# Merged additions for the compressed keys and values, and a different split of the PSUM banks, in a fused two-mixer transformer block

## The chip, the core and the metric

The kernel runs on one core of a Trainium2 chip. TensorE (PE in the profile) does the matrix multiplications and writes its results to PSUM, which has eight banks of 128 x 512 floats. VectorE (DVE) and ScalarE (ACT) read PSUM and do elementwise work, GpSimd (POOL) does elementwise work on SBUF alone, SyncE (SP) issues most DMAs. The metric is device time in microseconds (us), the median of several runs.

## The reference, cut to what matters

A block of x (512 tokens, width 1024) goes through a first mixer (an mLSTM branch and a stick-breaking attention branch), an MLP, and then a second mixer, "NSA": 16 heads of 64 in 4 key groups, and three attention branches (compressed, selected, window) that are gated and summed. The change lies in the second mixer. What it computes there:

```python
def compress_kv(kv, pos, w1, w2):        # 31 blocks of 32 tokens, one every 16 tokens
    blocks = kv[:, idx] + pos            # each block, plus a learned position table
    flat = blocks.reshape(B, n_cmp, G, CMP_BLOCK * dh)
    return jax.nn.silu(flat @ w1) @ w2   # done for the keys (k_c) and for the values (v_c)

kc, vc = compress_kv(k_c, ...), compress_kv(v_c, ...)
o_cmp, p_cmp = nsa_compressed(q, kc, vc, table)
o_slc = nsa_selected(q, k_s, v_s, sel, table)
o_win = nsa_window(q, k_w, v_w, table)
y = sum(gates * stack([o_cmp, o_slc, o_win]) * silu(z))   # z: three projections of width 1024
```

With 512 tokens the selected branch takes all 8 blocks and the window covers all tokens, so both are causal softmax attention over everything.

## The kernel before, in words

A float32 product is made of float32r parts: every operand is split into a high part and a remainder (`hi_lo`, or `Weights._load` for weights), and each product is three matmuls, high x high, low x high and high x low. In the trace a projection is therefore groups of three 128 x 512 matmuls on L339, L340 and L341 (`gen_t`, 24 matmuls into one PSUM bank), followed by `evac`, which reads the bank.

The second mixer (`nsa`) is written as an interleaving. `attention` walks through 8 head pairs, 2 branches, 2 heads and 4 blocks of queries. Each step issues the scores of one block (L1217 and L1218, into the ring of banks `sc`), then the transposes of an earlier block's probabilities ("flips", L1237, into the ring `tp`; ScalarE and VectorE copy them out to `ptall`), then the value product of a finished half (L1253, bank `av`). Between these a `Filler` puts pieces of other work, three matmuls at a time: the projections for the next queries, keys and the gates z (`project`, `queries`, `keys`), and the compressed branch (`compress`, `cmp_hidden`, `cmp_scores`, `cmp_flip`). These take their banks from `pj` or `mx`, which are one and the same ring, `bank`. The Filler's budget is counted in fixed costs, so the order of instructions on TensorE and GpSimd is settled when the program is built (`manual_schedule`); VectorE and ScalarE are ordered by the compiler's scheduler. All engines run in order.

A ring hands its banks out in turn, whoever asks. A matmul that opens a new tile in a bank waits until the last reader of the bank's previous tile is through. For a projection of z that reader is `evac` in `project`: ScalarE writes tanh(bank/2) to z (L995), then VectorE forms (z + 1) * bank (L296, in `stt`). For queries it is two ScalarE/VectorE pairs (L875 and L296).

`compress(i)` (i = 0 for keys, 1 for values) projects two 128-row halves, copies each to an SBUF tile (`kv`, L901), and while the next projection `project(0, i + 1)` runs, it builds four blocks F_ of shifted copies plus positions, eight additions of 64 x 4 x 31 each (`block`, L299 in `tt`), all eight at once at every second step. Each block is then split into Fh (ScalarE, L924) and Fl (GpSimd), and `cmp_hidden` multiplies the four (L942 to L944) into a bank of `pj`, interleaved with another projection by `both`.

Of the kernel before, what the change touches and what calls it, by code (L numbers as in the profile page):

```python
# [8 lines left out]
F32 = mybir.dt.float32  # L9
F32R = mybir.dt.float32r  # L10
# [5 lines left out]
T = 512  # L16
# [8 lines left out]
ZB = 5  # L25
# [220 lines left out]
def emit(gen):  # L246
    for _ in gen:
        pass
# [3 lines left out]
def tile_blocks(ctx, tc, x, xt, wts, prm, cst, table, post_g, w2k, w2v, out):  # L252
# [19 lines left out]
    ident = glob.tile([128, 128], F32, name="ident")  # L272
    ones = glob.tile([128, 128], F32, name="ones")
    v.memset(ones, 1.0)
    warm = glob.tile([128, 128], F32, name="warm", tag="dg", bufs=2)
    s.activation(warm, ones, AF.Identity, scale=ones[:, 0:1])
    wb = ring(7)()
    for _ in range(WARM):
        pe.matmul(wb[:, 0:128], ones, ones, start=True, stop=True)
    mhalf = glob.tile([128, 32], F32, name="mhalf")  # L280
# [34 lines left out]

    def row_broadcast(psum, r, name, scale=None):
        ps = psum()
        for tb in range(4):
            dg = glob.tile([128, 128], F32, name="dg", tag="dg", bufs=2)
            ts(dg, ident, r[:, tb:tb + 1])  # L320
            pe.matmul(ps[:, 128 * tb:128 * tb + 128], ones, dg, start=True, stop=True)
        o = glob.tile([128, T], F32, name=name, tag="rb", bufs=1)
        s.copy(o, ps)
        return o
# [70 lines left out]
    def first_mixer():  # L395
        with tc.tile_pool(name="pa", bufs=1) as pa:
            pj, sc, mx, tp, av = ring(0, 1, 2, 3), ring(4), ring(5), ring(6), ring(7)
            acts = []
# [18 lines left out]
            with tc.tile_pool(name="pm", bufs=1) as pm:  # L417
# [25 lines left out]
                with tc.issue_after(first.ins):  # L443
                    R = row_broadcast(mx, rs, "rbc")
                fa = pa.tile([8, T], F32, name="fa", tag="w2", bufs=2)
# [45 lines left out]
                for j in range(4):  # L491
# [16 lines left out]
                    for e in range(2):  # L508
# [33 lines left out]
                        for half in range(2):  # L542
# [7 lines left out]
                            v.tensor_copy(num[:, 2 * half:2 * half + 2, :], o2)  # L550
                        jk = glob.tile([128, 128], F32, name="jk", tag="dg", bufs=2)
                        for tb in range(4):
# [228 lines left out]
    def nsa(x2, ssq2):  # L781
# [4 lines left out]
        with ExitStack() as pts:  # L786
            pt = pts.enter_context(tc.tile_pool(name="pt", bufs=1))
            bank, sc, tp, av = ring(0, 1, 7), ring(2, 3), ring(4, 5), ring(6)

# [56 lines left out]

            def tmp(name="w"):
                return pt.tile([128, T], F32, name=name, tag="w", bufs=2)

            def keys_evac(gq):  # L850
                def evac(ps):
                    ks = tmp("ks")
                    s.copy(ks, ps)  # L853
                    for br in range(2):
                        kh = pn.tile([128, T], F32R, name="kh", tag="kh", bufs=4)
                        kl = pn.tile([128, T], F32R, name="kl", tag="kl", bufs=4)
                        src = ks[64 * br:64 * br + 64, :]
                        same = slice(64 * br, 64 * br + 64)
                        for d_ in range(2):
                            s.copy(kh[64 * d_:64 * d_ + 64, :], src)  # L860
                        for d_ in range(2):
                            tt(kl[64 * d_:64 * d_ + 64, :], src, kh[same, :].bitcast(F32), OP.subtract)
                        kst[gq, br] = (kh, kl)
                return evac
# [18 lines left out]
            def values(br):  # L883
                def evac(tb, ps):
                    src = ps[:, 0:256].rearrange("p (g d) -> p g d", g=4)
                    hi = vst[:, tb, 4 * br:4 * br + 4, 0:64]
                    gs = gn[:, tb, 24 * br:24 * br + 24]
                    s.activation(gs, ps[:, 256:280], AF.Tanh, scale=0.5)
                    ts(gs, gs, 0.25, 0.25, OP.mult, OP.add)
                    s.copy(hi, src)  # L890
                    tt(vst[:, tb, 4 * br:4 * br + 4, 64:128], src, hi.bitcast(F32), OP.subtract)
                emit(gen_n((ring(3, 4, 5, 6), ring(2, 0, 1, 7))[br], acts, evac, w=280))
                if br == 0:
                    ts(gn[:, 0, 0:16], gn[:, 0, 0:16], valid)

            def compress(i, hooks=((), ())):
                src = []

                def evac(ps):
                    t_ = tmp("kv")  # L900
                    s.copy(t_, ps)  # L901
                    src.append(t_)
                for m in range(2):
                    yield from weave(gen_t(pj, acts, evac), hooks[m])
                w2 = pt.tile([128, 2, 128 if i == 0 else 64], F32, name="w2", tag="pct", bufs=1)
# [3 lines left out]

                def block(j1, j2):  # L910
                    F_ = pt.tile([128, 4, 4, 32], F32, name="F_", tag="z", bufs=ZB)
                    tc.keep_in_program_order(g.memset(F_[:, :, :, 31:32], 0.0))
                    for gq in range(4):
                        r0 = 64 * (gq % 2)
                        kvv = src[gq // 2][r0:r0 + 64, :].rearrange("p (c j b) -> p b j c", j=8, b=2)
                        for jj in range(2):
                            p0 = base + 16 * jj + 8 * j1 + 4 * j2
                            tt(F_[64 * jj:64 * jj + 64, :, gq, 0:31],
                               kvv[:, jj, 4 * j2:4 * j2 + 4, j1:j1 + 31],
                               pr[r0:r0 + 64, p0:p0 + 4, None].to_broadcast([64, 4, 31]), OP.add)  # L920
                    Fh = pn.tile([128, 4, 128], F32R, name="Fh", tag="qy", bufs=QB)
# [3 lines left out]
                    tt(Fl, src_, Fh.bitcast(F32), OP.subtract, eng=g)  # L925
                    Fs.append((Fh, Fl))
                for k, ns in enumerate(project(0, i + 1)):
                    if k % 2 == 0:
                        block(k // 4, k // 2 % 2)
                    yield ns  # L930
# [22 lines left out]
            def cmp_middle(th):  # L953
                pst = mx()
                for k in range(2):
# [7 lines left out]
            def cmp_output(i, hT, w2):  # L963
                o = mx()
                for k in range(2):
# [8 lines left out]
                else:  # L974
                    vc = glob.tile([128, 128], F32, name="vc", tag="dg", bufs=2)[:, 0:64]
                    v.tensor_copy(vc, o[:, 0:64])
# [155 lines left out]
            def gate_flip(p):  # L1132
                pst = tp()
                for tb in range(4):
                    pe.transpose(pst[:, 128 * tb:128 * tb + 128], gz[:, 8 * tb:8 * tb + 128].bitcast(F32), ident)
                o = pt.tile([128, T], F32R, name="gT", tag="w", bufs=2)
                s.copy(o, pst)
# [124 lines left out]
            def attention(fill):  # L1262
# [70 lines left out]
                while pend_flip or pend_mix:  # L1333
# [6 lines left out]
            first = [(pj(), W.next(1), keys_evac(0)), (pj(), W.next(1), queries_evac(0)),  # L1340
                     (mx(), W.next(1), queries_evac(1))]
            enter(0)
# [110 lines left out]
```

## Time and profile before

| what | value |
|---|---|
| median of 3 runs | 1370.8 us (1369.51 to 1370.91) |
| the profiled execution | 1372.04 us, span 1370.3 us |
| PE busy, share of the span | 1324.2 us, 97% |
| DVE / ACT / POOL busy | 53% / 48% / 20% |

The profile lists the busy time of PE by stretch. Up to 430 us (first mixer) it is 415.4 us; from 430 to 875 us (mostly the MLP) 444.9 of 445; from 875 to 948 us (start of the second mixer) 69.7 of 73; from 948 to 1040 us (attention with the compressed branch) 78.8 of 92; from 1040 to 1330 us (attention with the remaining projections) 281.4 of 290; and in the last 40.3 us 33.9. PEclk is the TensorE clock that was granted: 1.00 is 2.4 GHz and 0.50 is 1.2 GHz.

A timeline row gives start (us from the span's start), duration in us, engine, line, operation, out<-in, sizes; in square brackets the idle time before it and what ended it. The names `b` are PSUM banks without their number.

### The profile page before, as it was taken

Reading aid. Unit: us, or ns where it says so; the run is one execution under the profiler, and the core shown is the slowest. Engines: PE = TensorE matmul, PEld = TensorE weight load, DVE = VectorE, ACT = ScalarE, POOL = GpSimd, SP = SyncE. Lnnn points to the kernel's source line nnn. Section 1 sums busy time; section 2 is a strip of 40 time slices with the busy share of each in tenths; the row PEclk is TensorE's granted clock in tenths of the full one; section 3 lists DMA queues with packets and bytes.
Section 4 is the critical chain, followed back from the end, with each engine's and each line's share of the span. In section 5 each row is a group of like instructions: output and inputs, shape, how many; then the busy total and the mean of one; then the engine's idle time right before and its main releaser. Section 6 shows DMA issues by size and latency. Waiting matters only on the chain.

```text
span 1370.3 us, 17904 instructions
## 1 busy us (share of the span) xinstructions
PE 1324.2 (97%) x6670; PEld 1090.5 (80%) x6670; DVE 728.0 (53%) x1386; ACT 656.0 (48%) x1281; POOL 273.7 (20%) x243
## 2 busy tenths in 40 slices
PE   9999999999999999999999999999888999999998
PEld 7977887777786888888888888888667788888776
DVE  4689435656567535342233322545785766665623
ACT  6588624544434326351135512355556556665532
POOL 0023101110101000000000000145536344335342
PEclk9999999999999999999999999999999999999999
DMA  7411221213131424863333324323313122211132
GB/s 236 139 46 49 76 93 55 85 62 93 51 103 47 155 61 133 125 183 94 96 102 93 95 94 129 118 64 119 94 55 111 52 63 62 70 62 63 47 108 77
DMA packets 40695, 125.31 MB, mean 91 GB/s; under 512 B 4528, under 2 KB 9184, under 8 KB 40352
## 3 DMA queue, kind: packets, MB, share of 16 engines
q1 hardware_dynamic: 39696, 119.98, 27.7%
q0 software_dynamic: 912, 4.19, 2.3%
q8 instruction: 52, 0.85, 0.3%
q14 instruction: 35, 0.29, 0.1%
HBM read 115.77 MB, written 8.39 MB: 91 GB/s over the span
## 4 chain that ended last, share of the span: by engine, by line
PE 66%; issue 15%; DVE 10%; ACT 5%; POOL 2%; DMA 1%; SPq 0%; POOLq 0%; DVEq 0%; ACTq 0%
PE b L374 9%; PE b L372 9%; PE b L373 9%; PE b L339 9%; PE b L340 9%; PE b L341 9%; PE b L1253 2%; PE b L1237 2%; DVE b L1220 1%; DVE ptall L299 1%; ACT P L1223 1%; PE b L1217 1%; PE b L828 1%; PE b L1218 1%; DMA xk<-in_xt_dram 1%
## 5 line engine op out<-in xcount | busy, mean ns | idle before, releaser
L171 ACT CAST wh<-wr 128x1024 fp32r<-128x1024 f32 (+3 forms) x204 | 207.8, 1019 | 403.1 <-PE b L374 225.6
L339 PE MATMUL b<-ah,wh 128*128 128x512 f32 x808 | 331.9, 411 | 2.8 <-ACT ks L853 2.4
L173 DVE TENSOR_TENSOR wl<-wr,wh 128x1024 fp32r<-128x1024 f32 (+2 forms) x142 | 169.5, 1195 | 296.9 <-ACT wh L171 296.4
L341 PE MATMUL b<-ah,wl 128*128 128x512 f32 x808 | 317.4, 393 | 0.0
L340 PE MATMUL b<-al,wh 128*128 128x512 f32 x808 | 317.0, 392 | 0.0
L173 POOL TENSOR_TENSOR wl<-wr,wh 128x1024 fp32r<-128x1024 f32 (+1 forms) x62 | 141.8, 2292 | 192.3 <-ACT wh L171 168.3
L341 PEld LDWEIGHTS b<-ah,wl 128*128 128x128 f32 x808 | 152.2, 188 | 32.4
L339 PEld LDWEIGHTS b<-ah,wh 128*128 128x128 f32 x808 | 152.6, 189 | 30.6 <-ACT ks L853 2.6
L340 PEld LDWEIGHTS b<-al,wh 128*128 128x128 f32 x808 | 152.8, 189 | 25.4 <-issue 1.9
L372 PE MATMUL b<-wh,ah 128*128 128x512 f32 (+3 forms) x352 | 125.5, 358 | 1.6 <-ACT wh L171 1.1
L373 PE MATMUL b<-wl,ah 128*128 128x512 f32 (+3 forms) x352 | 125.4, 356 | 0.1
L374 PE MATMUL b<-wh,al 128*128 128x512 f32 (+3 forms) x352 | 125.3, 356 | 0.1
L1223 ACT ACTIVATE P<-b,nm 128x128 f32<-128x128 f32 (+3 forms) x128 | 67.7, 529 | 80.3 <-DVE nm L1220 77.0
L374 PE MATMUL b<-wh,hl 128*128 128x512 f32 x256 | 101.2, 396 | 0.0
L373 PE MATMUL b<-wl,hh 128*128 128x512 f32 x256 | 101.2, 395 | 0.0
L372 PE MATMUL b<-wh,hh 128*128 128x512 f32 x256 | 101.2, 395 | 0.0
L299 DVE TENSOR_TENSOR ptall<-b,ptall 128x128 fp32r<-128x128 f32 (+3 forms) x128 | 62.5, 489 | 62.3 <-ACT ptall L1240 61.4
L1220 DVE CUSTOM_DVE_ANT_0 b<-b,bt 128x128 f32<-128x128 f32 (+3 forms) x128 | 63.1, 494 | 24.4 <-PE b L1218 24.2
L372 PEld LDWEIGHTS b<-wh,ah 128*128 128x128 f32 x352 | 66.2, 188 | 9.9 <-ACT wh L171 1.3
L374 PEld LDWEIGHTS b<-wh,al 128*128 128x128 f32 x352 | 66.4, 189 | 8.4 <-DVE al L296 0.5
L373 PEld LDWEIGHTS b<-wl,ah 128*128 128x128 f32 x352 | 66.4, 189 | 8.4 <-DVE wl L173 0.5
L299 POOL TENSOR_TENSOR rsr<-rsm,mhalf 128x2 f32<-128x2 f32 (+1 forms) x3 | 2.4, 806 | 336.1 <-DVE rsm L293 336.1
(301 smaller groups left out, 2163.7 us busy)
## 6 DMA issues: line engine op xcount, KB each, us to landing
wr<-in_wts_dram SPq DMA_DIRECT2D x188, 512.0 KB, 3.6
bt_d<-tr POOLq DMA_DIRECT2D x4, 768.0 KB, 21.9
wr<-in_wts_dram SPq DMA_DIRECT2D x8, 280.0 KB, 2.6
xk<-in_xt_dram SPq DMA_DIRECT2D x8, 256.0 KB, 3.8
xn<-in_x_dram SPq DMA_DIRECT2D x4, 512.0 KB, 4.7
xbig<-in_x_dram SPq DMA_DIRECT2D x1, 2048.0 KB, 9.4
x_d<-xbig SPq DMA_DIRECT2D x8, 256.0 KB, 3.1
bt<-bt_d SPq DMA_DIRECT2D x8, 256.0 KB, 3.2
```

Of the source, the lines that this page charges most:

```text
L171: nc.scalar.copy(hi, raw)
L173: eng.tensor_tensor(lo, raw, hi.bitcast(F32), OP.subtract)
L299: (eng or v).tensor_tensor(out_, a, b, op)
L339: pe.matmul(o, a, ah, start=(kt == 0), stop=False)
L340: pe.matmul(o, a, al, start=False, stop=False)
L341: pe.matmul(o, b, ah, start=False, stop=(kt == KT - 1))
L372: pe.matmul(o, ah[:, tsl], a, start=(kk == 0 and k == 0), stop=False)
L373: pe.matmul(o, ah[:, tsl], b, start=False, stop=False)
L374: W.last = pe.matmul(o, al[:, tsl], a, start=False, stop=end)
L1220: v.tensor_tensor_reduce(S[:, 0:n], S[:, 0:n], self.bt[:, h % 2, 512 - n:512], 1.0, -NEG, OP.add, OP.min, nm)
L1223: latest[0] = s.activation(P[:, 0:n], S[:, 0:n], AF.Exp, bias=nm, scale=-1.0, accum_out=self.dn[:, tb, br, h % 2:h % 2 + 1])
L1237: pe.transpose(pst[:, 128 * sb:128 * sb + 128], P[:, 128 * sb:128 * sb + 128], ident)
```

## The change

Three things change, and some tiles move.

1. The banks of the second mixer are dealt out differently. Before, `pj`/`mx` have banks 0, 1 and 7 and `tp` has 4 and 5. After, `pj`/`mx` have 0 and 1, and `tp` has 4, 5 and 7. `cmp_middle` and `cmp_output` take their bank from `tp` now, the third of the first projections takes bank 6, and the two `values` projections use other sets of four.
2. The two `kv` halves are kept in one tile `w2t`, so one addition covers the two key groups that lie on the same 64 rows: 64 x 8 x 31 in place of two of 64 x 4 x 31, and 32 additions in all where there were 64.
3. These are issued two at each of the eight steps of the projection, not eight at every second step.

`ones`, the warm-up matmuls and the tiles `dg`, `jk` move from the pool that lives throughout into the first mixer's pool; `vc` becomes a slice of `w2t`; `gT` gets a buffer of its own.

```diff
-            bank, sc, tp, av = ring(0, 1, 7), ring(2, 3), ring(4, 5), ring(6)
+            bank, sc, tp, av = ring(0, 1), ring(2, 3), ring(4, 5, 7), ring(6)
...
-            def tmp(name="w"):
-                return pt.tile([128, T], F32, name=name, tag="w", bufs=2)
+            w2t = pt.tile([128, 2, T], F32, name="w2t")
...
-                emit(gen_n((ring(3, 4, 5, 6), ring(2, 0, 1, 7))[br], acts, evac, w=280))
+                emit(gen_n((ring(3, 4, 5, 7), ring(2, 0, 1, 6))[br], acts, evac, w=280))
...
                 for m in range(2):
-                    yield from weave(gen_t(pj, acts, evac), hooks[m])
+                    yield from weave(gen_t(pj, acts, lambda ps, m=m: s.copy(w2t[:, m, :], ps)), hooks[m])
...
-                def block(j1, j2):
-                    F_ = pt.tile([128, 4, 4, 32], F32, name="F_", tag="z", bufs=ZB)
-                    tc.keep_in_program_order(g.memset(F_[:, :, :, 31:32], 0.0))
-                    for gq in range(4):
-                        r0 = 64 * (gq % 2)
-                        kvv = src[gq // 2][r0:r0 + 64, :].rearrange("p (c j b) -> p b j c", j=8, b=2)
-                        for jj in range(2):
-                            p0 = base + 16 * jj + 8 * j1 + 4 * j2
-                            tt(F_[64 * jj:64 * jj + 64, :, gq, 0:31],
-                               kvv[:, jj, 4 * j2:4 * j2 + 4, j1:j1 + 31],
-                               pr[r0:r0 + 64, p0:p0 + 4, None].to_broadcast([64, 4, 31]), OP.add)
+                def block(j1, j2, part, F_):
+                    if part == 0:
+                        F_ = pt.tile([128, 4, 4, 32], F32, name="F_", tag="z", bufs=ZB)
+                        tc.keep_in_program_order(g.memset(F_[:, :, :, 31:32], 0.0))
+                    odd = part
+                    r0 = 64 * odd
+                    kvv = w2t[r0:r0 + 64, :, :].rearrange("p g (c j b) -> p b j g c", j=8, b=2)
+                    for jj in range(2):
+                        p0 = base + 16 * jj + 8 * j1 + 4 * j2
+                        tt(F_[64 * jj:64 * jj + 64, :, odd:4:2, 0:31],
+                           kvv[:, jj, 4 * j2:4 * j2 + 4, :, j1:j1 + 31],
+                           pr[r0:r0 + 64, p0:p0 + 4, None, None].to_broadcast([64, 4, 2, 31]), OP.add)
+                    if part == 0:
+                        return F_
...
+                F_ = None
                 for k, ns in enumerate(project(0, i + 1)):
-                    if k % 2 == 0:
-                        block(k // 4, k // 2 % 2)
+                    F_ = block(k // 4, k // 2 % 2, k % 2, F_)
                     yield ns
...
             def cmp_middle(th):
-                pst = mx()
+                pst = tp()
...
             def cmp_output(i, hT, w2):
-                o = mx()
+                o = tp()
...
-                     (mx(), W.next(1), queries_evac(1))]
+                     (av(), W.next(1), queries_evac(1))]
```

The instructions of TensorE, GpSimd and SyncE come in the same order before and after; on TensorE only the banks and the waits differ. These are its rows before, at the place where the first z projection of head pair 1 ends and the second begins (b0, b7 and so on are banks with the number of the tile in them, wh and wl a weight's two parts, kh and kl keys, ah and al the activations, P the probabilities):

```order
L339 MATMUL b0_8785<-ah7_6869,wh_8570 128x512
L340 MATMUL b0_8785<-al7_6870,wh_8570 128x512
L341 MATMUL b0_8785<-ah7_6869,wl_8571 128x512
L1217 MATMUL b2_8886<-kh_7274,q_7192 128x128 [waits Activation_49]
L1218 MATMUL b2_8886<-kl_7275,q_7192 128x128
L339 MATMUL b7_8900<-ah0_6855,wh_8623 128x512
L340 MATMUL b7_8900<-al0_6856,wh_8623 128x512
L341 MATMUL b7_8900<-ah0_6855,wl_8624 128x512 [waits Pool_49]
L1237 MATMUL b5_8904<-ident_65,P_8804 128x128 [waits DVE_49]
```

And after, at the same place; the changed file's lines are numbered lower by 7 for the helpers and by 4 further down:

```order
L332 MATMUL b0_8746<-ah7_6869,wh_8533 128x512
L333 MATMUL b0_8746<-al7_6870,wh_8533 128x512
L334 MATMUL b0_8746<-ah7_6869,wl_8534 128x512
L1213 MATMUL b2_8847<-kh_7273,q_7192 128x128 [waits Activation_49]
L1214 MATMUL b2_8847<-kl_7274,q_7192 128x128
L332 MATMUL b0_8861<-ah0_6855,wh_8586 128x512 [waits DVE_49]
L333 MATMUL b0_8861<-al0_6856,wh_8586 128x512
L334 MATMUL b0_8861<-ah0_6855,wl_8587 128x512 [waits Pool_49]
L1233 MATMUL b5_8865<-ident_65,P_8765 128x128 [waits PE_49]
```

The second projection opened a tile in bank 7 with no wait, and now opens one in bank 0, the bank of the projection that has just ended, and waits for VectorE; the scores of the compressed branch had taken bank 1 in between, in both versions.

VectorE before, in the first `compress`, from the flip of one block of probabilities to the copy of another (F_ are the blocks, ptall the copied-out flips, rows L1220 the maximum over the scores):

```order
L299 TENSOR_TENSOR ptall<-b_7749,ptall 128x128
L299 TENSOR_TENSOR F__7756<-kv,pr 64x4x31 x7
L1220 ISA b_7775,nm<-b_7775,bt 128x128
L1220 ISA nm 128x1
L299 TENSOR_TENSOR F__7785<-kv,pr 64x4x31 x8
L299 TENSOR_TENSOR ptall<-b_7799,ptall 128x2x128
L299 TENSOR_TENSOR F__7827<-kv,pr 64x4x31
L1220 ISA b_7817,nm<-b_7817,bt 128x256
L1220 ISA nm 128x1
L299 TENSOR_TENSOR F__7827<-kv,pr 64x4x31 x2
```

And after, the same stretch:

```order
L292 TENSOR_TENSOR ptall<-b_7742,ptall 128x128
L292 TENSOR_TENSOR F__7749<-w2t,pr 64x8x31 x4
L1216 ISA b_7764,nm<-b_7764,bt 128x128
L1216 ISA nm 128x1
L292 TENSOR_TENSOR F__7774<-w2t,pr 64x8x31 x2
L292 TENSOR_TENSOR ptall<-b_7778,ptall 128x2x128
L292 TENSOR_TENSOR F__7774<-w2t,pr 64x8x31 x2
L1216 ISA b_7802,nm<-b_7802,bt 128x256
L1216 ISA nm 128x1
L292 TENSOR_TENSOR t_7568<-t_7568,b_7721 64x512
L292 TENSOR_TENSOR F__7812<-w2t,pr 64x8x31 x2
```

Fewer additions stand between two of the attention's instructions: at most four where there were eight. In both versions all additions of a block stand ahead of the projection's last eviction on VectorE.

## Rows read from the trace of the kernel before

**Rows 1.** windows view: PE busy (x), PEld, DVE, ACT, POOL, PEclk, DMA share, GB/s.

```profile
960.00:1040.00 80.00, 66.86 (x384) 56.00 (x385) 60.59 (x147) 44.44 (x104) 38.95 (x28) 0.96 0.25 77
1040.00:1330.00 290.00, 281.42 (x1597) 236.37 (x1597) 180.91 (x458) 171.39 (x421) 121.98 (x70) 0.99 0.23 71
```

**Rows 2.** waits of PE, 1040 to 1330 us: total us, times, longest.

```profile
PE b L339 <- ACT ks L853: 2.4, 1, 2.4
PE b L1237 <- DVE ptall L299: 1.9, 5, 0.7
PE b L1135 <- DVE ptall L299: 1.8, 1, 1.8
```

**Rows 3.** windows view of the granted clock (PEclk) behind four pauses of PE.

```profile
975.20:978.50 3.30, 3.29 (x10) 2.53 (x11) 2.56 (x8) 2.42 (x7) 3.15 (x2) 0.50 0.00 0
1029.90:1033.10 3.20, 3.20 (x13) 2.82 (x12) 0.42 (x1) 1.85 (x5) 3.20 (x2) 0.50 0.24 45
1057.80:1061.00 3.20, 3.20 (x20) 2.86 (x21) 2.86 (x4) 3.13 (x6) 1.91 (x1) 1.00 0.09 24
1316.60:1319.80 3.20, 3.20 (x13) 2.72 (x11) 1.86 (x3) 0.59 (x1) 2.55 (x2) 0.50 0.46 92
```

**Rows 4.** timeline around 1067.9 us: start, us, engine, line, out<-in.

```profile
1067.46 0.39 PE L341 MATMUL b<-ah,wl 128*128 128x512 f32 x1
...
1067.87 0.45 PE L339 MATMUL b<-ah,wh 128*128 128x512 f32 x1
...
1067.97 1.06 ACT L171 CAST wh<-wr 128x1024 fp32r<-128x1024 f32 x1
...
1068.92 0.61 ACT L995 ACTIVATE z<-b 128x512 f32<-128x512 f32 x1
...
1069.56 0.69 DVE L296 SCALAR_TENSOR_TENSOR z<-z,b 128x512 f32<-128x512 f32 x1 [0.89 <-ACT z L995]
```

**Rows 5.** timeline at the first and the last of fourteen such places.

```profile
1046.69 0.48 PE L339 MATMUL b<-ah,wh 128*128 128x512 f32 x1
...
1047.17 0.69 DVE L296 SCALAR_TENSOR_TENSOR q<-b,q 64x512 fp32r<-64x512 f32 x1 [0.22 <-ACT q L875]
...
1292.54 0.48 PE L339 MATMUL b<-ah,wh 128*128 128x512 f32 x1
...
1294.36 0.69 DVE L296 SCALAR_TENSOR_TENSOR z<-z,b 128x512 f32<-128x512 f32 x1
```

**Rows 6.** timeline of VectorE: additions of a block, and three evictions.

```profile
972.73 1.84 DVE L299 TENSOR_TENSOR F__7827<-kv,pr 64x124 f32<-64x124 f32 x5
...
975.55 0.68 DVE L296 SCALAR_TENSOR_TENSOR z<-z,b 128x512 f32<-128x512 f32 x1
...
991.37 0.68 DVE L296 SCALAR_TENSOR_TENSOR z<-z,b 128x512 f32<-128x512 f32 x1
...
1026.93 0.69 DVE L296 SCALAR_TENSOR_TENSOR z<-z,b 128x512 f32<-128x512 f32 x1
```

**Rows 7.** groups of instructions after 740 us: xcount, busy us, mean ns of one.

```profile
L299 DVE TENSOR_TENSOR Pc<-b,Pc 128x256 f32<-128x256 f32 x16 | 6.7, 418 | 1.2 <-PE b L1050 0.9
...
L299 DVE TENSOR_TENSOR Pc<-Pc,rgc 128x512 f32<-128x512 f32 x4 | 2.8, 692 | 0.1
```

**Rows 8.** timeline of PE around the three hidden-layer and following places.

```profile
970.30 0.37 PE L942 MATMUL b<-wh,Fh 128*128 128x256 f32 x1
...
972.75 0.38 PE L1253 MATMUL b<-ptall,vst 128*128 128x256 f32 x1 [0.78 <-DVE t L299]
...
975.21 0.47 PE L1237 MATMUL b<-ident,P 128*128 128x128 f32 x1 [1.27 <-DVE ptall L299]
...
989.47 0.47 PE L339 MATMUL b<-ah,wh 128*128 128x512 f32 x1
...
1022.81 0.36 PE L942 MATMUL b<-wh,Fh 128*128 128x256 f32 x1
...
1028.28 0.33 PE L1135 MATMUL b<-ident,gz 128*128 128x128 f32 x1 [3.48 <-DVE ptall L299]
```

More of the change, by code (lines that the diff above doesn't have):

```diff
@@ L272, in tile_blocks @@
     ident = glob.tile([128, 128], F32, name="ident")
[L273 to L279, printed above, removed]
     mhalf = glob.tile([128, 32], F32, name="mhalf")
@@ L314, in rsqrt_mean, with row_broadcast @@
         return r
-    def row_broadcast(psum, r, name, scale=None):
+    def row_broadcast(psum, r, name, pa, ones):
         ps = psum()
         for tb in range(4):
-            dg = glob.tile([128, 128], F32, name="dg", tag="dg", bufs=2)
+            dg = pa.tile([128, 128], F32, name="dg", tag="dg", bufs=2)
             ts(dg, ident, r[:, tb:tb + 1])
@@ L396, in first_mixer @@
         with tc.tile_pool(name="pa", bufs=1) as pa:
+            ones = pa.tile([128, 128], F32, name="ones")
+            v.memset(ones, 1.0)
+            warm = pa.tile([128, 128], F32, name="warm", tag="dg", bufs=2)
+            s.activation(warm, ones, AF.Identity, scale=ones[:, 0:1])
+            wb = ring(7)()
+            for _ in range(WARM):
+                pe.matmul(wb[:, 0:128], ones, ones, start=True, stop=True)
             pj, sc, mx, tp, av = ring(0, 1, 2, 3), ring(4), ring(5), ring(6), ring(7)
@@ L443, in first_mixer @@
                 with tc.issue_after(first.ins):
-                    R = row_broadcast(mx, rs, "rbc")
+                    R = row_broadcast(mx, rs, "rbc", pa, ones)
                 fa = pa.tile([8, T], F32, name="fa", tag="w2", bufs=2)
@@ L550, in first_mixer @@
                             v.tensor_copy(num[:, 2 * half:2 * half + 2, :], o2)
-                        jk = glob.tile([128, 128], F32, name="jk", tag="dg", bufs=2)
+                        jk = pa.tile([128, 128], F32, name="jk", tag="dg", bufs=2)
                         for tb in range(4):
@@ L845, in nsa @@
             fill = Filler()
-            def tmp(name="w"):
-                return pt.tile([128, T], F32, name=name, tag="w", bufs=2)
+            w2t = pt.tile([128, 2, T], F32, name="w2t")
             def keys_evac(gq):
                 def evac(ps):
-                    ks = tmp("ks")
+                    ks = w2t[:, 0, :]
                     s.copy(ks, ps)
@@ L896, in compress @@
             def compress(i, hooks=((), ())):
[L897 to L902, printed above, removed]
                 for m in range(2):
-                    yield from weave(gen_t(pj, acts, evac), hooks[m])
+                    yield from weave(gen_t(pj, acts, lambda ps, m=m: s.copy(w2t[:, m, :], ps)), hooks[m])
                 w2 = pt.tile([128, 2, 128 if i == 0 else 64], F32, name="w2", tag="pct", bufs=1)
@@ L974, in cmp_output @@
                 else:
-                    vc = glob.tile([128, 128], F32, name="vc", tag="dg", bufs=2)[:, 0:64]
+                    vc = w2t[:, 1, 0:64]
                     v.tensor_copy(vc, o[:, 0:64])
@@ L1135, in gate_flip @@
                     pe.transpose(pst[:, 128 * tb:128 * tb + 128], gz[:, 8 * tb:8 * tb + 128].bitcast(F32), ident)
-                o = pt.tile([128, T], F32R, name="gT", tag="w", bufs=2)
+                o = pt.tile([128, T], F32R, name="gT", tag="gT", bufs=1)
                 s.copy(o, pst)
```

## The prediction

> **What bounds the kernel now.** I read first the busy shares by stretch, then what TensorE waits for, then the granted clock behind its pauses, then the single places. TensorE works for nearly the whole span: of 1040 to 1330 us it idles only 290 - 281.4 = 8.6 us, and the one loose stretch is 960 to 1040 us with 80 - 66.9 = 13.1 us [rows 1]. In that stretch the compressed branch's additions crowd VectorE. So the most that shorter waits can give is these 21.7 us and what the clock takes; a new wait of TensorE, on the other hand, lands on the span in full.
>
> The waits after 1040 us are of two kinds [rows 2]. Flips and gate matmuls (L1237, L1135) wait for a bank of `tp` to be read out. And once, for 2.4 us, a projection (L339) waits for a bank whose last reader is the copy of the keys (L853): there the ring `bank` had come round to a bank that had just been filled. That row is the price of what the change does often.
>
> A pause of TensorE can cost twice, because the clock may halve behind it [rows 3]. Behind the pauses that end at 975.2 us, 1028.3 us and 1314.5 us a stretch of some 3.3 us was granted 0.50 (1.2 GHz instead of 2.4); behind the one of 2.4 us that ends at 1057.8 us the clock stayed at 1.00. TensorE is busy throughout such a stretch, so it costs half of it, about 1.7 us.
>
> **The change part by part.**
>
> *Two banks for projections.* In the order of the changed kernel, the compressed branch's scores and flips take a bank between two projections. With three banks the next projection still found an empty one. With two it gets the bank of the projection that has just ended, and waits until its eviction is through. How long is read from the trace of before, since TensorE's order is the same. At one such place the last matmul of the old projection ends at 1067.46 + 0.39 = 1067.85, and the next starts at 1067.87 [rows 4]. ScalarE is then busy with the cast of the next weights, which begins as the projection ends (1067.97, 1.06 us); tanh follows at 1068.92, and VectorE's z ends at 1069.56 + 0.69 = 1070.25. New wait: 1070.25 - 1067.87 = 2.38 us. I paired in this way every tile with the last reader of its new bank's previous tile: after 1040 us there are fourteen places where the reader ends later than the matmul starts. The first is 1047.17 + 0.69 - 1046.69 = 1.17 us, the last 1294.36 + 0.69 - 1292.54 = 2.51 us [rows 5]; eleven of them are at 1.8 us or more, the largest is 3.2 us, and the fourteen make 31.7 us. They don't overlap: each is some 10 us from the next, and in between TensorE is the bound [rows 1]. What is queued behind a waiting matmul is all of TensorE: flips, scores, value products. ScalarE and VectorE run dry behind it, and nothing makes up for it.
>
> *Three banks for flips, and a freed key bank.* With bank 7 in `tp` its waits after 1040 us go: at each of them the bank now used had been read out earlier. The key wait of 2.4 us goes too, since the projection there now gets the other bank. I count all 8.6 us of [rows 1] as gained.
>
> *Merged, dealt-out additions.* An addition of 64 x 4 x 31 takes 1.84 / 5 = 0.37 us [rows 6]. One with twice the elements is not in the trace. An addition of 256 elements per row takes 0.42 us and one of 512 takes 0.69 us [rows 7], so 124 more elements are worth 0.27 x 124 / 256 = 0.13 us: 0.50 us. Bounds: 0.42 us (the 256-element row) and 0.74 us (twice 0.37, if the pattern of strides is the limit). I take 0.50, the nearer row's slope. In the first block stretch 27 additions lie behind the second copy of the halves; they become 16, since a merged addition needs both halves and so none can start early: 27 x 0.37 - 16 x 0.50 = 2.0 us less. In the second stretch it is 26, so 1.6 us less.
>
> What these 2 us are worth depends on the bank again. The first hidden-layer matmul started at 970.30 us without waiting for a bank [rows 8]. Now its bank is that of the projection whose z is formed behind all sixteen additions: 975.55 + 0.68 = 976.23 [rows 6], less 2.0, makes 974.2. That is 3.9 us later than 970.30; the 0.78 and 1.27 us that TensorE lost just behind [rows 8] go. Net 1.9 us lost. In the second stretch: 1026.93 + 0.69 = 1027.62, less 1.6, makes 1026.0 against 1022.81, 3.2 us later, and the 3.48 us behind it [rows 8] go: 0.3 us won. Between them a projection started at 989.47 [rows 8] into a bank that is now read out only at 991.37 + 0.68 = 992.05 [rows 6]: 2.6 us lost. Together 4.2 us lost. Bounds: if VectorE, with its work dealt out, were never late, the 13.1 us of the stretch and two half-clock stretches would go, 16.5 us won, less 2.6; if an addition takes 0.74 us, 16 x 0.24 = 3.8 us more are lost in each stretch, 12 in all.
>
> *The clock.* Before, of three single pauses of 1.8 us or more (3.5, 2.4 and 1.8), two had a half-clock stretch behind them. New pauses of 1.8 us or more: eleven after 1040 us and the one at 989 us. At two in three, eight more stretches; the one of 1316 us goes with its pause. 7 x 1.7 = 11.9 us lost. Bounds: none behind the new pauses (1.7 won) and one behind each (11 x 1.7 = 18.7 lost).
>
> The Trainium skill, "TensorE: Matmul & The Clock Gate", section "A second HAM failure mode: psum-queue depth-cycling", speaks against the change: in a kernel that cycled through PSUM banks, TensorE paused briefly between groups so often that its clock went down and up again and again. The trace shows single cases of it, two of three pauses. By that page the upper bound, 18.7 us, would stand in the sum instead of 11.9.
>
> *The rest at nothing.* The warm-up and its tiles move, with TensorE's order unchanged; the single tile `w2t`, the slice for `vc` and the single `gT` are written again only long after their last reader; the other banks for `values` shift one wait by less than half a microsecond. If that cover were gone, a wait on one of them would be another eviction of 1 to 2 us.
>
> **Sum.** 31.7 - 8.6 + 4.2 + 11.9 = 39.2 us on the profiled execution's 1372.0 us: 1411.2. That execution is 1.2 us above the median of the runs, so 1410 us.
>
> **The rivals.**
>
> *The pauses come, the clock holds.* For it: the pause of 2.4 us at 1057.8 us, the only one in the trace that is exactly of the new kind, had full clock behind it. Against: two of three. 31.7 - 8.6 + 4.2 - 1.7 = 25.6: 1396 us.
>
> *A half-clock stretch behind every pause.* For it: the pause of 1.8 us had one. Against: that of 2.4 us. 31.7 - 8.6 + 4.2 + 18.7 = 46: 1417 us. By the skill's section named above it is this one.
>
> *The merged additions cost twice the single ones,* so that the change doesn't do what it says: 8 us more than forecast, 1418 us. For it: one operand is read in a long stride. Against: the slope of contiguous additions.
>
> *Faster, since the bank comes free early.* The mechanism is the eviction's place in ScalarE's queue. If tanh ran ahead of the weight cast, 0.61 + 0.69 us and 0.1 of handing over make 1.4 us behind the last matmul; less the matmuls that lie between at most places, the fourteen waits would make 13.4 us and none would be long enough for the clock. With the additions dealt out so well that the 16.5 us are won too: 13.4 - 8.6 - 16.5 - 1.7 = -13.4, so 1357 us. It decides from the point where the fourteen cost under about 1.9 us each, with the early stretch at its best bound. For it: ScalarE is free half of the time. Against: the cast starts as the projection's last weights come free, which is just ahead of tanh, and on ScalarE's order it still stands there.
>
> **How the numbers follow.** Forecast 0.55; clock holds 0.20; stretch behind every pause 0.10; additions at twice the cost 0.06; faster 0.07; no change 0.02. About 0.2% is what a measurement of this kernel can tell from no change, 2.7 us. Faster 0.07, same 0.02, slower 0.91. The range reaches down below the rival in which the clock holds, with some of the early stretch won, 1387 us, and up to just over the two worse ones, 1422 us.
>
> **What would show it.** In the profile after, TensorE should wait on L332 (the first matmul of a projection) for the z of L289 on VectorE at some dozen places for over 2 us each, 25 us and more in all, and it should show up at L938 in the first block stretch. The waits of the flips (L1233) and gate matmuls (L1131) for `ptall` should be nearly gone. The additions should be 32 of about 0.5 us. Half-clock stretches should number about ten between 960 and 1330 us, where there were three. The forecast is wrong if the projections' waits come to under 15 us, or if the clock shows as few half stretches as before.

## The result: 1423.8 us, and the profile after

The changed kernel took 1423.81 us (median of 4 runs, 1423.39 to 1424.4) against 1370.44 us, a ratio of 1.0389 with a 95% interval of 1.0377 to 1.0402: 53.4 us slower, where 39 were forecast, and 1.8 us above the range. The direction and the place were right; the size wasn't.

The loss splits in two. Busy time of TensorE, on the page of the kernel after (busy us, share of the span, instructions, for each engine):

```profile
PE 1342.8 (94%) x6670; PEld 1107.0 (78%) x6670; DVE 727.8 (51%) x1354; ACT 658.5 (46%) x1281; POOL 273.4 (19%) x243
```

With the same 6670 matmuls, busy time rose from 1324.2 to 1342.8 us, 18.6 us more, and idle time from 1370.3 - 1324.2 = 46.1 to 1421.6 - 1342.8 = 78.8 us, 32.7 more. Together this is 51.3 us, the whole difference of the spans. Idle time is waits; more busy time for the same matmuls is the clock.

The waits of PE after, from 930 us to the end (total us, times, longest us):

```profile
PE b L332 <- DVE z L289: 28.0, 13, 2.8
PE b L938 <- DVE z L289: 12.5, 2, 6.6
PE b L332 <- DVE q L289: 3.4, 1, 3.4
PE b L1076 <- issue: 3.1, 1, 3.1
PE b L1213 <- ACT P L1219: 3.1, 2, 2.7
PE b L1249 <- DVE t L292: 2.6, 3, 1.0
PE b L1131 <- DVE gz L292: 1.9, 1, 1.9
```

The first row is the forecast one: a projection's first matmul (L332) waits for the z of L289. The key wait, the flips' waits and the gate flip's wait of [rows 2] are gone. The 1.9 us of L1131 are not that wait but a new one, at another gate flip: before, the first and the last of the eight waited (at 1028.28 and 1314.53 us); now the second does (at 1054.23), for `gz`, which it flips. What made `gz` late stands in the last section.

The timeline after, at the first block stretch and at the place of [rows 4] (start, us, engine, line, operation):

```profile
955.13 2.40 POOL L173 TENSOR_TENSOR wl<-wr,wh 128x1024 fp32r<-128x1024 f32 x1 [5.12 <-ACT wh L171]
...
956.13 2.36 DVE L292 TENSOR_TENSOR F__7717<-w2t,pr 64x248 f32<-64x248 f32 x2 [2.01 <-ACT w2t L897]
...
972.38 1.14 DVE L292 TENSOR_TENSOR F__7812<-w2t,pr 64x248 f32<-64x248 f32 x2
...
974.14 0.68 DVE L289 SCALAR_TENSOR_TENSOR z<-z,b 128x512 f32<-128x512 f32 x1
...
974.88 0.58 PE L938 MATMUL b<-wh,Fh 128*128 128x256 f32 x1 [5.87 <-DVE z L289]
...
1080.17 0.28 PE L1214 MATMUL b<-kl,q 128*128 128x128 f32 x1
...
1080.69 1.06 ACT L171 CAST wh<-wr 128x1024 fp32r<-128x1024 f32 x1
...
1081.63 0.61 ACT L991 ACTIVATE z<-b 128x512 f32<-128x512 f32 x1
...
1082.27 0.69 DVE L289 SCALAR_TENSOR_TENSOR z<-z,b 128x512 f32<-128x512 f32 x1 [0.89 <-ACT z L991]
...
1083.02 0.55 PE L332 MATMUL b<-ah,wh 128*128 128x512 f32 x1 [2.57 <-DVE z L289]
```

The last five rows are [rows 4] again, with one difference: there the next projection started at once, here it starts behind the z at 1082.96. Cast, tanh, z: the forecast chain, 2.57 us instead of 2.38. In the block stretch the hidden layer's first matmul (L938) waits 5.87 us for a z that ends at 974.82; 974.2 was forecast.

The windows view after: the two stretches of [rows 1], up to a later end, and six stretches at half clock (columns as there, PEclk is the third number from the right):

```profile
960.00:1040.00 80.00, 61.28 (x339) 52.58 (x338) 51.53 (x109) 41.22 (x96) 34.84 (x25) 0.85 0.21 66
1040.00:1380.00 340.00, 304.24 (x1635) 254.59 (x1634) 191.56 (x467) 177.04 (x429) 123.72 (x72) 0.93 0.20 61
...
967.30:981.00 13.70, 7.83 (x31) 6.53 (x30) 8.84 (x18) 6.63 (x14) 6.96 (x5) 0.50 0.12 38
1028.70:1038.90 10.20, 5.40 (x23) 5.21 (x24) 6.13 (x14) 5.49 (x14) 6.46 (x5) 0.50 0.14 45
1056.00:1062.80 6.80, 4.26 (x11) 3.52 (x12) 4.01 (x10) 3.52 (x8) 3.24 (x2) 0.50 0.40 134
1083.30:1086.70 3.40, 3.40 (x13) 2.75 (x12) 0.42 (x1) 0.37 (x1) 0.94 (x1) 0.50 0.36 110
1097.00:1103.80 6.80, 6.27 (x17) 5.00 (x18) 2.01 (x6) 0.83 (x3) 2.70 (x2) 0.50 0.28 80
...
1223.30:1230.10 6.80, 5.99 (x20) 5.21 (x21) 1.80 (x5) 2.20 (x5) 3.65 (x2) 0.50 0.31 80
```

After 1040 us TensorE idles 340 - 304.2 = 35.8 us where it idled 8.6, at a mean clock of 0.93 instead of 0.99. Behind a pause, or from inside it (1028.7, 1097.0, 1223.3), the grant falls to 0.50, 1.2 GHz. Six more stretches of some 3.4 us at 0.50, beside the one at 1083.3, begin at 1124.3, 1137.9, 1264.2, 1308.6, 1322.3 and 1346.1 us. That makes twelve from 960 to 1360 us, 68 us together; before there were three of some 3.4 us [rows 3].

### The profile page after: what moved, and what is told of

Read it like the earlier page. It is cut to its first block, busy times and chain, and to the rows that moved or that the text cites. A ratio compares the mean times of both kernels' runs of the same rounds, so it can differ in the third digit from the quotient of the medians.

```text
span 1421.6 us, 17886 instructions
## 1 busy us (share of the span) xinstructions
PE 1342.8 (94%) x6670; PEld 1107.0 (78%) x6670; DVE 727.8 (51%) x1354; ACT 658.5 (46%) x1281; POOL 273.4 (19%) x243
## 4 chain that ended last, share of the span: by engine, by line
PE 67%; issue 15%; DVE 10%; ACT 4%; POOL 2%; DMA 1%; DVEq 0%; POOLq 0%; SPq 0%; ACTq 0%
PE b L332 10%; PE b L333 9%; PE b L334 9%; PE b L367 9%; PE b L365 9%; PE b L366 9%; PE b L1249 2%; PE b L1233 2%; DVE b L1216 1%; PE b L1213 1%; PE b L1214 1%; PE b L828 1%; DMA xk<-in_xt_dram 1%; ACT wh L171 1%; ACT P L1219 1%
## 5 line engine op out<-in xcount | busy, mean ns | idle before, releaser
L332 PE MATMUL b<-ah,wh 128*128 128x512 f32 x808 | 337.0, 417 | 32.1 <-DVE z L289 28.0
L334 PE MATMUL b<-ah,wl 128*128 128x512 f32 x808 | 321.5, 398 | 0.0
L333 PE MATMUL b<-al,wh 128*128 128x512 f32 x808 | 321.0, 397 | 0.0
L332 PEld LDWEIGHTS b<-ah,wh 128*128 128x128 f32 x808 | 154.6, 191 | 63.8 <-DVE z L289 31.4
L1236 ACT CAST ptall<-b 128x128 fp32r<-128x128 f32 (+3 forms) x128 | 54.0, 423 | 30.7 <-PE b L1233 29.8
```

The costliest lines, as they stand in the source:

```text
L332: pe.matmul(o, a, ah, start=(kt == 0), stop=False)
L333: pe.matmul(o, a, al, start=False, stop=False)
L334: pe.matmul(o, b, ah, start=False, stop=(kt == KT - 1))
```

## The experiments

All are timed against the kernel before in shared runs; its median was 1370.2 or 1370.3 us there and 1370.4 beside the changed kernel, so the times can be set side by side. Idle is the span less TensorE's busy time, both of the profiled execution; before it was 46.1 idle and 1324.2 busy, after 78.8 and 1342.8.

| kernel | us | ratio (95%) | idle | busy |
|---|---|---|---|---|
| e1 after, old banks | 1370.48 | 1.0005 (0.9996 to 1.0015) | 46.2 | 1325.2 |
| e8 e1, additions not dealt out | 1368.95 | 0.9992 (0.9983 to 1.0001) | 44.3 | 1325.9 |
| e2 before, new banks | 1420.0 | 1.0370 (1.0353 to 1.0387) | 78.5 | 1338.0 |
| e3 after, two takers moved to `tp` | 1375.39 | 1.0038 (1.0024 to 1.0053) | 51.7 | 1323.0 |
| e4 after, bank emptied by one copy | 1401.86 | 1.0233 (1.0219 to 1.0246) | 68.2 | 1331.7 |
| e5 after, eleven pauses filled | 1411.04 | 1.0298 (1.0283 to 1.0313) | 60.2 | 1348.9 |
| e6 before, oldest bank first | 1366.17 | 0.9969 (0.9958 to 0.9981) | 40.5 | 1321.9 |
| e7 after, oldest bank first | 1366.5 | 0.9976 (0.9967 to 0.9985) | 43.1 | 1321.7 |

My theory: the loss is the ring of two banks, through waits for evictions and through the clock behind them. The rivals: the merged, dealt-out additions do part of it; two banks are too few for any order; the clock's share is small.

**The two parts apart: e1, e2 and e8.** e1 keeps the additions of the change and takes the bank split back:

```diff
-            bank, sc, tp, av = ring(0, 1), ring(2, 3), ring(4, 5, 7), ring(6)
+            bank, sc, tp, av = ring(0, 1, 7), ring(2, 3), ring(4, 5), ring(6)
...
-                pst = tp()
+                pst = mx()
...
-                o = tp()
+                o = mx()
```

with the rings of `values` and the bank of the third projection as before. 

> The changed kernel with the bank split of the kernel before (three for projections, two for flips), so that only the merged and dealt-out additions are left. Theory (the two-bank ring makes the whole loss): TensorE no longer waits for z at the projections after 1040 us and no bank wait stands at the first hidden-layer matmul; half-clock stretches fall back to three or fewer; time 1362 to 1371 us, at or a little under before. Rival (starting all additions only behind the second half, and dealing them out, costs by itself): over 1378 us, with VectorE later than before in the stretch of 960 to 1040 us.

e2 puts the new bank split into the kernel before. 

> The kernel before with the new bank split alone; its 64 additions stay as they were. Theory (the ring makes the loss, the merged additions are worth almost nothing beside it): 1420 to 1430 us, with the same dozen waits for z. Rival (the two parts together make the loss, as the merged additions lie behind the bank wait): under 1405 us.

e8 is e1 with the merged additions issued four at every second step:

```diff
-                    F_ = block(k // 4, k // 2 % 2, k % 2, F_)
+                    if k % 2 == 0:
+                        F_ = block(k // 4, k // 2 % 2, 0, F_)
+                        block(k // 4, k // 2 % 2, 1, F_)
```

> The kernel with the old bank split and merged additions, issued four at once at every second step and not two at each. Theory (VectorE is the bound there, so the order of its additions hardly matters): within 3 us of the run with the old banks, 1367 to 1374 us. Rival (dealing out is what eats the gain of merging): 1365 us or less.

e2 alone is 49.8 us slower than the kernel before, e1 can't be told from it, nor can e8. So the banks make the loss; merged additions, dealt out or not, are worth nothing that these intervals show (e8, the better of the two, can be 2.3 us under before at most). Why nothing, when VectorE has half as many? The waits of PE from 948 to 1045 us, in the kernel before and then in e1:

```profile
PE b L1237 <- DVE ptall L299: 5.7, 7, 1.6
PE b L1135 <- DVE ptall L299: 3.5, 1, 3.5
PE b L1253 <- DVE t L299: 2.3, 2, 1.5
PE b L1217 <- ACT P L1223: 1.6, 1, 1.6
```

```profile
PE b L1213 <- ACT P L1219: 5.5, 4, 2.5
PE b L1131 <- DVE ptall L292: 4.0, 1, 4.0
PE b L1233 <- DVE ptall L292: 2.2, 3, 1.1
PE b L1249 <- DVE t L292: 1.2, 2, 0.8
```

They sum to 12.9 us in e1 and to 13.1 before. The flips wait less, but the scores wait 3.9 us more for P, whose maximum queues among the additions on VectorE; and the gate flip that waited 3.48 us [rows 8] waits 4.0. VectorE in e1 ahead of it:

```profile
1023.37 3.16 DVE L292 TENSOR_TENSOR F__8349<-w2t,pr 64x248 f32<-64x248 f32 x4
...
1027.28 0.68 DVE L289 SCALAR_TENSOR_TENSOR z<-z,b 128x512 f32<-128x512 f32 x1
```

z starts at 1027.28, where it started at 1026.93 [rows 6]. What counts is the additions behind the second copy of the halves, and there the merging saved hardly anything: summed over their rows, 27 took 12.98 us before and 16 take 13.00 in e1 in the first stretch, 26 took 12.91 and 16 take 12.23 in the second. The rest of the saving lies with additions that ran early before.

After is 3.8 us over e2, but the intervals of the two overlap, and the four runs of e2 reach from 1418.2 to 1424.0 us, so a cost of the merged additions on top of the banks isn't shown. The two profiled executions differ in the clock: idle time is the same (78.8 and 78.5), busy time is 4.8 us lower in e2, and it has 51 us at half speed instead of 68, with the same count of twelve stretches.

**Two banks, or who takes them: e3.** In the kernel after, two short-lived takers that stand between projections move to the ring of three:

```diff
 # cmp_scores
-                S = mx()
+                S = tp()
...
 # cmp_flip
-                pst = mx()
+                pst = tp()
```

> The changed kernel, with the compressed branch's scores and flips taking their bank from the flips' ring (4, 5, 7) and not from the projections' two, so that projections alternate 0, 1, 0, 1. Theory (not the number of banks but the taker in between makes a projection meet the bank that has just been filled): the waits after 1060 us go, 25.6 us for z and 3.1 us at L1076, and with them nine or so half-clock stretches, about 12 us; what stays are the waits at the two hidden layers, at 993 us and at 1055 us; time 1378 to 1390 us. Rival (two banks are too few whoever takes them, since an eviction takes as long as the work between two projections): over 1405 us.

It came out 2.6 us below the range. 48.4 of the 53.4 us are gone with two banks for projections still. All its waits of PE from 1060 us on:

```profile
PE b L1249 <- DVE t L292: 1.7, 2, 0.9
PE b L1141 <- DVE ptall L292: 0.6, 1, 0.6
```

No projection waits there any more. Two banks that alternate are enough; another taker between two projections turns the ring by one, and the next projection meets the bank just filled. What stays, 5 us over the kernel before, lies ahead of 1060 us: the two hidden layers, which still take a bank of that ring and wait for z (5.2 and 6.6 us), and two projections (2.3 us for z at 994, 3.3 us for q at 1056).

**Is the wait the eviction's length: e4.** For all but the first three projections of z a copy empties the bank, and tanh and product read the copy:

```diff
                 def evac(ps):
-                    s.activation(z, ps, AF.Tanh, scale=0.5)
-                    stt(z, z, 1.0, ps, OP.add, OP.mult)
+                    zc = ps
+                    if p > 0:
+                        zc = w2t[:, 0, :]
+                        v.tensor_copy(zc, ps)
+                    s.activation(z, zc, AF.Tanh, scale=0.5)
+                    stt(z, z, 1.0, zc, OP.add, OP.mult)
```

> The changed kernel with another eviction of the gate projections of head pairs 1 to 7: VectorE first copies the bank to SBUF, and tanh and the product read the copy, so the bank is free after one instruction that doesn't queue behind ScalarE's weight cast. Theory (what a projection waits for is the length of the eviction in front of it): the waits at the eleven places shrink from 2.4 us to about 1.3 us each, 12 us in all, most half-clock stretches behind them go, and the time falls to 1395 to 1412 us, although VectorE has 21 copies more to do. Rival (the wait is set by VectorE's backlog): the waits stay over 2 us and the time at 1420 us or more.

Measured 1401.86, inside. The place of [rows 4] in e4's timeline:

```profile
1079.94 0.27 PE L1218 MATMUL b<-kl,q 128*128 128x128 f32 x1
...
1080.80 0.68 DVE L994 COPY w2t<-b 128x512 f32<-128x512 f32 x1
...
1081.54 0.50 PE L332 MATMUL b<-ah,wh 128*128 128x512 f32 x1 [1.33 <-DVE w2t L994]
...
1081.64 2.40 POOL L173 TENSOR_TENSOR wl<-wr,wh 128x1024 fp32r<-128x1024 f32 x1 [8.75 <-ACT wh L171]
...
1082.18 2.41 DVE L289 SCALAR_TENSOR_TENSOR z<-z,w2t 128x512 f32<-128x512 f32 x1 [0.43 <-ACT z L995]
```

The matmul now starts behind the copy, 1.33 us late instead of 2.57. Idle time fell by 10.6 us and busy time by 11.1: the shorter waits gave as much again in clock, although e4's profiled execution has a half-clock stretch at 7.7 us, far ahead of the change, that after's has not.

**The clock's share by itself: e5.** Ahead of eleven of the waiting projections, eight matmuls whose result nobody reads go into a bank of `tp`, so that TensorE works through the pause:

```diff
+                if (p, br) in ((1, 1), (1, 2), (2, 2), (2, 0), (3, 2), (4, 2),
+                               (4, 0), (5, 1), (6, 2), (6, 0), (7, 1)):
+                    d = tp()
+                    for _ in range(8):
+                        pe.matmul(d, acts[0][0][:, 0:128], acts[0][0], start=True, stop=True)
                 yield from gen_t(pj, acts, evac)
```

> The changed kernel with eight matmuls of 128 x 512, whose results nobody reads, ahead of each of the eleven z projections that wait for their bank: the wait stays, but TensorE works for 1.7 us of it. Theory (beyond the pauses themselves the clock makes the rest of the loss): the half-clock stretches behind those eleven places go, from twelve between 960 and 1360 us to four or five, and the time falls by 8 to 14 us, to 1410 to 1416 us, although TensorE has 19 us more to do. Rival (the loss beyond the pauses comes from queues on VectorE and ScalarE): 1423 us or more.

12.8 us faster than after, with 88 matmuls more. One filled pause in e5's timeline:

```profile
1079.71 0.27 PE L1218 MATMUL b<-kl,q 128*128 128x128 f32 x1
1079.83 2.04 PE L996 MATMUL b<-ah 128*128 128x512 f32 x8
1082.56 0.50 PE L332 MATMUL b<-ah,wh 128*128 128x512 f32 x1 [0.69 <-DVE z L289]
```

The projection starts as late behind its predecessor as ever (2.6 us), and the clock behind it, in e5's windows view, is whole:

```profile
1082.90:1086.30 3.40, 3.40 (x23) 2.95 (x22) 1.05 (x4) 1.02 (x3) 0.90 (x1) 1.00 0.45 114
```

What one of the longer stretches costs can be read from the next such place, from the projection's first matmul to the value product behind it, first in after and then in e5:

```profile
1097.53 0.79 PE L332 MATMUL b<-ah,wh 128*128 128x512 f32 x1 [2.69 <-DVE z L289]
...
1103.98 0.28 PE L1249 MATMUL b<-ptall,vst 128*128 128x256 f32 x1
```

```profile
1095.50 0.50 PE L332 MATMUL b<-ah,wh 128*128 128x512 f32 x1 [0.84 <-DVE z L289]
...
1099.06 1.04 PE L1253 MATMUL b<-ptall,vst 128*128 128x256 f32 x8
```

The same 17 matmuls took 6.45 us, nearly all at half clock, and 3.56 at the full one: 2.9 us more. Half-clock time falls to 34 us. In busy time: a filling matmul follows the last at about 0.23 us (the eight take 2.04, the last of them 0.39), so 88 are about 20 us; 1348.9 - 20 = 1329, against 1342.8. So about 14 of the 18.6 us are the clock behind these eleven places; the rest lies around the pauses that weren't filled, in the block stretch and after it (six half-clock stretches are left, three of them behind 1040 us).

**A better bank order: e6 and e7.** The five banks of the two rings go into one list, and a taker gets the one released longest ago; a projection releases its bank when its eviction is issued, a short-lived taker at once:

```diff
-            bank, sc, tp, av = ring(0, 1, 7), ring(2, 3), ring(4, 5), ring(6)
+            sc, av = ring(2, 3), ring(6)
+            order, held = [0, 1, 7, 4, 5], {}
+            def grab():
+                i = order.pop(0)
...
+            def drop(t_):
+                order.append(held.pop(id(t_))[0])
+            def brief():
+                t_ = grab()
+                drop(t_)
+                return t_
+            tp = brief
```

e6 does this to the kernel before, e7 to the one after. 

> The kernel before (64 additions) with no fixed split: projections, flips and hooks take, from the five banks 0, 1, 4, 5 and 7, the one whose eviction was issued longest ago, and a projection gives its bank back when its eviction is issued. Theory (the loss and the small waits of the kernel before are both a matter of which bank is met): waits for banks after 1040 us nearly vanish, some 8 us, and part of the 13 us before them; time 1354 to 1364 us, faster than both kernels. Rival (five banks are too few for two projections and the flips at once, whatever the order): 1368 us or more.

> The changed kernel (32 merged additions, dealt out) with banks taken as in the run with the oldest bank. Theory: as that one within 4 us, 1352 to 1364 us, since VectorE stays the bound of the stretch around 960 to 1040 us with either form of the additions. Rival (merging pays once no bank is in the way): 6 us or more under the run with the oldest bank and 64 additions.

Both beat the kernels they come from: e6 by 4 us, 0.3%, with an interval that stays below 1, e7 by 57. e6 is still 2 us above its range, and e7 2.5 us above its own. The waits of PE in e6 from 1040 to 1330 us:

```profile
PE b L339 <- DVE q L296: 3.3, 1, 3.3
PE b L1277 <- DVE t L299: 1.8, 2, 1.0
PE b L1159 <- DVE q L296: 0.9, 1, 0.9
```

The flips' waits are gone, and of the projections one still waits, 3.3 us for the queries' eviction. That wait alone is longer than the miss. The eviction is late there because VectorE stood for 2.31 us in a small subtraction for `gz` ahead of it (1040.30 us; see the last section); why the list hands out just that bank isn't shown. e7 and e6 differ by 0.3 us, less than their runs tell apart: the merged additions show no worth here either.

## Why the prediction was wrong, point by point

**The bank waits: right, with one offset.** 31.7 us forecast for fourteen places. Measured: 28.0 of L332 behind z, less the one of 2.35 us at 993 us, which was counted with the block stretch, plus 3.4 behind q and the 3.1 of L1076: 32.2. Pairing each tile with its bank's previous reader in the old trace gave number and place, and the sum. One place is far off: the first, behind q, waited 3.35 us where 1.17 were forecast, for the reason in the last section, and the other thirteen came to 28.8 where 30.5 were.

**The old waits gone: right, but new ones came, 3.7 us.** 8.6 us were taken as gained, and every wait behind them is gone. What the forecast put at nothing are new waits outside the two rings: `gz` is late for the second gate flip (1.86 us), and two value products (L1249) wait 0.97 and 0.82 us for t, which is formed from the bank `av`.

**The block stretch: the sum near, its parts not.** Loss of 4.2 forecast; idle time from 948 to 1045 us rose by 5.6 us, from 13.1 to 18.7. The merging was to save 2.0 and 1.6 us behind the second copy; after's rows sum to 12.93 and 12.24 us where 12.98 and 12.91 stood, so it saved under 0.1 and 0.7. An addition was taken at 0.50 us and took 0.57 where nothing disturbed it (1.14 / 2 above), and the time in which additions stood still beside GpSimd, 3 to 4 us in each stretch, was there before and stayed (last section). That the first z ended at 974.82, near the 974.2, is luck: the second copy ended 1.45 us earlier than before (956.10 and 957.55). The hidden layers' waits came to 12.5 us where 3.9 + 3.2 were forecast; the sum stayed near because more of the stretch's old waits went than the 5.5 us that were counted.

**The clock: the step that failed.** "At two in three, eight more stretches ... 7 x 1.7 = 11.9 us" was the term; busy time shows 18.6 us. Two sizes in it were wrong. The share: of the twelve pauses of 1.8 us or more after 1040 us, only the one of 2.38 us at 1149.8 has no half-clock stretch behind it, and the two at 1052 and 1055 share one; the pause of 2.35 us at 993, which the forecast counted too, has none. From 960 to 1360 us there are nine stretches more than before, not seven. The two of three that I had were too few to set a rate by. The price: a stretch was taken as 3.4 us of half-speed work, after single pauses in the old trace. Five of the twelve last two to four times as long, partly filled by the pause itself; the one measured above cost 2.9 us, not 1.7. The rival with a stretch behind every pause had 18.7 us for this term, as measured, but by luck: it counted eleven stretches more, of 1.7 us each. Its 1417 us was short by the other terms. The Trainium skill, "TensorE: Matmul & The Clock Gate", section "A second HAM failure mode: psum-queue depth-cycling", speaks for that rival: cycling through PSUM banks with frequent short idle times makes the clock go up and down. The trace agrees, with ten such stretches after 1040 us, and e5 shows the price: 12.8 us net come back when the same waits are filled.

With these in place the sum is 32.2 - 8.6 + 3.7 + 5.6 + 18.6 = 51.5, the spans' 51.3. Of the 12.3 us that the forecast's 39.2 lacks, the clock is 6.7, the new waits 3.7, the block stretch 1.4 and the bank waits 0.5. The other 1.6 us of the distance to 1423.8 come from the profiled executions, which lay above the median before and below it after.

**The other rivals.** The clock did not hold. The additions did not double, with 0.57 us against 0.37. Faster fell: ScalarE ran the weight cast ahead of tanh, as in [rows 4].

What stays open: which pause draws a half-clock stretch, and how long a one. A pause of 2.57 us drew 3.4 us, one of 2.69 drew 6.8, one of 2.38 none. It isn't the pause's length alone: behind 1060 us e2 has after's pauses, all but one to 0.02 us, yet the one of 2.76 us at 1219, which drew 6.8 us in after, drew none there, nor did the one of 2.40 at 1121, which drew 3.4. With about the same waits, 32.4 and 32.7 us, the clock's term was 13.8 us in e2's execution and 18.6 in after's. No experiment varied a pause by itself.

## What to carry to other kernels

A ring of PSUM banks is judged by who stands between two long holders, not by its length: a short taker in the same ring makes two projections meet in one bank (1423.8 us), the same two banks without it don't (1375.4), and taking the bank released longest ago is better than both (1366.5 with the same additions). The Trainium skill, "Perfetto Trace Analysis", section "Matmuls", says that independent groups of matmuls should rotate through different banks so that one's eviction overlaps the next; the 2.57 us above are what it costs where they don't. And where TensorE is the bound, a repeated pause of about 2 us costs more than itself, for the clock behind it: here 32.7 us of waits cost 18.6 more, 32.4 us in e2 13.8 more, and e4 got 11.1 us of clock back with 10.6 us of waits.

## What the runs showed that was not expected

In these traces an elementwise operation with two operands in SBUF stands still on VectorE while GpSimd subtracts; with one operand in PSUM it doesn't. At the place of [rows 4], z<-z,b took 0.69 us in the kernel after, though GpSimd was forming `wl` (1081.87, 2.37 us). In e4 the same product read the copy instead of the bank, and took 2.41 us beside GpSimd's 2.40. Over all projections, in the groups by form, first after and then e4 (count, busy us, mean ns):

```profile
L289 DVE SCALAR_TENSOR_TENSOR z<-z,b 128x512 f32<-128x512 f32 x24 | 16.5, 686 | 16.0 <-ACT z L991 16.0
```

```profile
L289 DVE SCALAR_TENSOR_TENSOR z<-z,w2t 128x512 f32<-128x512 f32 x21 | 33.3, 1584 | 10.0 <-ACT z L995 9.6
```

In e4 five of the 21 had no GpSimd subtraction beside them and took 0.69 us each; the other sixteen took 0.98 to 2.41 us, fourteen of them just the time that lay beside the subtraction plus 0.55 us. The additions suffer from it too: the first two merged ones took 2.36 us, beside the `wl` of 955.13, where the two at 972.38 took 1.14. The Trainium skill, "SBUF — State Buffer", section "SBUF: two separate sides", states it as an exclusive lock of a port pair that VectorE and GpSimd share, taken, among others, by an operation with two SBUF inputs; these rows agree. Merging took the additions' sum from 33.7 to 25.1 us in the two stretches, but not that part: behind the second copy, what the disturbed ones took over an undisturbed one came to 6.9 us before and 6.8 after.

It also made the late `gz`. Rows of after, VectorE beside two subtractions of GpSimd's, and one of before:

```profile
1049.34 4.71 POOL L173 TENSOR_TENSOR wl<-wr,wh 128x1024 fp32r<-128x1024 f32 x2
...
1049.45 2.32 DVE L1122 CAST gz<-gs 128x16 fp32r<-128x16 f32 x1
1051.81 2.27 DVE L292 TENSOR_TENSOR gz<-gs,gz 128x16 fp32r<-128x16 f32 x1
```

```profile
1042.62 0.18 DVE L299 TENSOR_TENSOR gz<-gs,gz 128x16 fp32r<-128x16 f32 x1
```

Two operations on 16 columns took 4.6 us in place of 0.35, and one of them, the cast, has a single operand. Before, GpSimd began its next `wl` at 1042.90 us, just behind them. The gate flip waited 1.86 us for `gz`, and the queries' eviction, queued behind it, made the next projection wait 2.2 us longer than forecast. So some 4 us of the loss come from a meeting of VectorE and GpSimd that the shifted times brought about; e1, with the old banks, has neither wait.
